# Gate and up products of a SwiGLU block by Strassen's algorithm, and the FFN walked group by group

## The chip, the core and the metric

The kernel runs on one core of a Trainium2 chip. TensorE (PE) multiplies, VectorE (DVE), ScalarE (ACT) and GpSimd (POOL) work elementwise, and transfers between HBM and the on-chip memory are issued by SyncE (SP). The metric is the device time of one execution in microseconds (us); the time of a kernel is the median of several runs.

## The reference, cut to what matters

One layer of a hybrid encoder: 2048 tokens, model width 1024, FFN width 2816 (22 blocks of 128). The first part (projections, two kinds of attention, a short convolution) is left alone by the change, but for the sizes of some buffers. The second part, on which the change works, is

```
x = x + y @ w_out[l]
x = x + swiglu(rmsnorm(x, ffn_norm_w[l]), w_gate[l], w_up[l], w_down[l])

def swiglu(x, w_gate, w_up, w_down):
    return (jax.nn.silu(x @ w_gate) * (x @ w_up)) @ w_down
```

## The kernel before

Tokens are handled in 4 groups of 512, in two halves of two groups. Every float32 product is made of three matmuls on split operands: high by high, high by low and low by high (`mm3`, L379 to L381). For the projections and for gate and up the parts are float16; for `w_down` they are float32r.

First comes a woven stage (`weave`, `fill`): projections, attention and the output projection of the first half are interleaved on TensorE by a clock of estimated costs. Then `ffn(0)` runs the FFN of the first half, `out_proj` the output projection of the second half with nothing beside it, and `ffn(1)` the FFN of the second half.

Within `ffn` the 22 FFN blocks f are taken two at a time. For each f and each of the half's two groups g, `hidden` (L379 to L381) makes gate and up: 8 slices of the width 1024, three matmuls each, with a 128x128 piece of the weight as the stationary operand and 512 tokens as the moving one, into a PSUM bank `acc`. ScalarE reads gate (`silu`, L1034), VectorE multiplies by up (`gated`, L1038), and the result is split into `gh` (ScalarE, L1041) and `gl` (VectorE, L1042). One pair later `down` (L1057 to L1059) multiplies these by `w_down`: six matmuls of 512 columns for each bank `sc`, of which there are three, and VectorE adds the bank to the residual `x1` (L1061). Weights of gate and up are scaled, cast and split once in `ffn(0)` (L249, L274 to L276) and stored as float16 in HBM (`wd`), from where `ffn(1)` fetches them (L236). `w_down` is loaded and split in each half (`load_down`, L310 to L314).

The order on TensorE is the order in which the program is written; in the FFN, and on the other engines everywhere, a scheduler sets it. All DMAs go through SP's one queue, in order.

Of the kernel before, what the change touches and what calls it, by code (L numbers as in the profile page):

```python
# [9 lines left out]
F32 = mybir.dt.float32  # L10
# [8 lines left out]
D = 1024  # L19
# [16 lines left out]
def f32(ap):  # L36
    return ap.bitcast(F32)
# [3 lines left out]
def trunk(ctx: ExitStack, tc: tile.TileContext, x, anw, w_in, qnw, knw, biasx, conv_w, onw, w_out,  # L41
# [17 lines left out]
    wp = ctx.enter_context(tc.tile_pool(name="wp", bufs=8))  # L59
    xp = ctx.enter_context(tc.tile_pool(name="xp", bufs=6))  # L60
# [109 lines left out]
    def block(key):  # L170
# [13 lines left out]
        if key[0] == "gu":  # L184
            return SH_T, False, "f", [cols(w, every, 128 * key[1], 128) for w in (w_gate_k, w_up_k)]
# [121 lines left out]
    def load_down(f, low):  # L307

        raw = wp.tile([128, D], F32, name="wr", tag="wr", bufs=4)
        nc.sync.dma_start(raw, w_down[f * 128:(f + 1) * 128, :])  # L310
        hi = wp.tile([128, D], F32R, name="wh", tag="w16")
        nc.scalar.copy(hi, raw)
        lo = wp.tile([128, D], F32R, name="wl", tag="w16")
        low.tensor_tensor(lo, raw, f32(hi), ALU.subtract)  # L314
        return hi, lo
# [5 lines left out]
    def to_T(xn, hh, hl, t):  # L321

        cs = slice(t * 128, (t + 1) * 128)
        for i in range(2):
            p, bk = sc1()
# [15 lines left out]
    def gain_row(key):  # L341

        w = {"a": anw, "o": onw, "f": fnw}[key]
        gt = xp.tile([128, D], F32, name="gain", tag="gain", bufs=1)
        nc.sync.dma_start(gt, bass.AP(tensor=w.tensor, offset=w.offset, ap=[[0, 128], [1, D]]))
        if key not in GS:
# [6 lines left out]
            nc.vector.tensor_scalar(t, t, -1.0, float(2 * 127 + 9), op0=ALU.mult, op1=ALU.add)  # L353
# [155 lines left out]
    def proj_N(H, groups, units, use, prep=None):  # L509

        for g in groups:
            hh, hl = H.get(g, (None, None))
            for t in range(0, 4, 2):
# [3 lines left out]
                o, bk = acc()  # L517
# [192 lines left out]
    def open_av():  # L710
        return bank("av", 1, 2 * HD)
# [146 lines left out]
    def out_proj(H, groups, W, prep, rows):  # L858

        for g in groups:  # L860
            for cb in range(4):
# [13 lines left out]
                if g == groups[-1] and cb in (1, 2) and len(groups) > 1:  # L875
                    yield from rows.ahead()

    def ffn_rows(H, groups):
        def fetch(g, b):
            xt = xp.tile([128, D], F32, name="xf", tag="xt")  # L880
            last_row[where(g)[0]] = nc.sync.dma_start(xt, x1d[g * 4 + b])
            return xt

        return Rows(H, groups, fetch, normed("f"))

    HF = [{}, {}]
    last_row = [None, None]
    frows = [ffn_rows(HF[i], groups) for i, groups in enumerate(HALVES)]


# [8 lines left out]

    def fill():  # L900
# [3 lines left out]
        rows = [x_rows(H[0], HALVES[0]), x_rows(H[1], HALVES[1]), y_rows(H[2], HALVES[0])]  # L904
        for half, groups in enumerate(HALVES):
# [19 lines left out]
        yield from out_proj(H[2], HALVES[0], W, rows[2], frows[0])  # L925
# [4 lines left out]
    FFN = [("gu", f) for f in range(NF)]  # L930
    stream = Weights(HALF * 2 + OUT * len(HALVES[0]) + FFN + OUT * len(HALVES[1]) + FFN)
    def hidden(u, h):

        (wh, wl), (hh, hl) = u, h
        o, bk = acc()
        bk.done = True
        yield from mm3(o, lambda k: wh[:, k, :], lambda k: wl[:, k, :], lambda k: hh[:, k, :],
                       lambda k: hl[:, k, :], KT)
        return o

# [77 lines left out]
    fp = ctx.enter_context(tc.tile_pool(name="fp", bufs=1))  # L1018

    def ffn(half, groups):  # L1020
        X1 = {}
        H = HF[half]

        def product(u, g):
            steps = hidden(u, H[g])
            while True:
                try:
                    next(steps)
                except StopIteration as e:
                    return e.value  # L1030

        def silu(f, o):
            sg = fp.tile([128, GRP], F32, name="sg", tag="sg", bufs=3)
            nc.scalar.activation(sg, o, AF.Silu, scale=descale(("gu", f), 0))  # L1034
            return sg

        def gated(f, sg, o):
            nc.vector.scalar_tensor_tensor(sg, o, descale(("gu", f), 1), sg, op0=ALU.mult, op1=ALU.mult)  # L1038
# [101 lines left out]
```

## Time and profile before

| | |
|---|---|
| median of 3 runs (lowest, highest) | 2697.33 us (2696.89, 2701.96) |
| the profiled execution | 2698.59 us, of which the trace's span is 2696.8 us |
[...]
| TensorE busy, share of the span | 94% |
| VectorE, ScalarE, GpSimd | 54%, 40%, 15% |

The span is the time from the first to the last instruction. A matmul's time in the trace covers its way through the pipeline and overlaps the next one's, so what a matmul costs in a stream is the distance between the starts of successive ones.

### The profile page before, as it was taken

The numbers are of one execution on the slowest core, as the hardware profiler recorded it, in microseconds if no ns is written. First come the engines' busy times: TensorE is split into PE (matmuls) and PEld (weight loads), VectorE is DVE, ScalarE is ACT, GpSimd is POOL, SyncE is SP. The second block draws the span as 40 slices with busy tenths as digits, with TensorE's granted clock in tenths as the row PEclk, the third lists the DMA queues.
The fourth block names the chain that finished last, engine by engine and source line by source line (L and its number), as shares of the span: only waits on it lengthen the run. The fifth ranks groups of instructions, "written<-read, shape, count | busy, mean of one in ns | idle before, by whom it ended". The sixth has DMA issues, their size and how long they took to land.

```text
span 2696.8 us, 41816 instructions
## 1 busy us (share of the span) xinstructions
PE 2526.3 (94%) x16258; PEld 1687.1 (63%) x16258; DVE 1458.7 (54%) x3343; ACT 1074.8 (40%) x1994; POOL 398.8 (15%) x469
## 2 busy tenths in 40 slices
PE   6998889998799888979999999999999999999999
PEld 4477766666686677745555555557865555555556
DVE  6478777689988977834444334334332333223233
ACT  5575756666456776752333333321121111111110
POOL 2234331102312122121111111110000000000000
PEclk9999999999999999989999999999999999999999
DMA  7443444533321356472222233222651111111101
GB/s 260 133 131 100 132 134 143 142 110 124 105 81 43 97 152 198 120 268 105 94 94 94 94 103 113 90 102 107 223 194 39 47 47 51 66 47 48 47 24 63
DMA packets 245350, 294.31 MB, mean 109 GB/s; under 512 B 77472, under 2 KB 194208, under 8 KB 245152
## 3 DMA queue, kind: packets, MB, share of 16 engines
q1 hardware_dynamic: 245152, 291.65, 33.5%
q8 instruction: 127, 2.08, 0.3%
q14 instruction: 71, 0.58, 0.1%
HBM read 199.30 MB, written 92.27 MB: 108 GB/s over the span
## 4 chain that ended last, share of the span: by engine, by line
PE 38%; DMA 4%; issue 4%; DVE 2%; POOL 1%; ACT 1%; SPq 1%; POOLq 0%; DVEq 0%; ACTq 0%
PE acc L381 7%; PE acc L380 7%; PE acc L379 7%; PE sc L1057 5%; PE sc L1058 5%; PE sc L1059 5%; DMA x1d<-xs 1%; POOL w L276 1%; DMA wr<-in_w_down 1%; DMA wr<-in_w_up 1%; DMA xf<-x1d 0%; PE sc L329 0%; DVE gl L1042 0%; DVE x L1061 0%; DVE wl L314 0%
## 5 line engine op out<-in xcount | busy, mean ns | idle before, releaser
L381 PE MATMUL acc<-hh,w 128*128 128x512 f16 x1728 | 656.3, 380 | 0.8 <-POOL w L276 0.8
L379 PE MATMUL acc<-hh,w 128*128 128x512 f16 x1728 | 656.5, 380 | 0.4 <-ACT hh L332 0.4
L380 PE MATMUL acc<-hl,w 128*128 128x512 f16 x1728 | 656.4, 380 | 0.1
L1038 DVE SCALAR_TENSOR_TENSOR sg<-acc,ds,sg 128x512 f32<-128x512 f32 x88 | 66.0, 750 | 622.9 <-PE acc L381 548.8
L379 PE MATMUL acc<-w,hh 128*128 128x256 f16 x1408 | 391.6, 278 | 5.8 <-ACT w L275 4.2
L380 PE MATMUL acc<-w,hh 128*128 128x256 f16 x1408 | 391.5, 278 | 1.8 <-POOL w L276 1.8
L381 PE MATMUL acc<-w,hl 128*128 128x256 f16 x1408 | 391.0, 278 | 1.5 <-DVE hl L333 0.8
L1061 DVE TENSOR_TENSOR x<-sc,x 128x512 f32<-128x512 f32 x352 | 241.2, 690 | 200.9 <-PE sc L1059 194.1
L381 PEld LDWEIGHTS <-w 128*128 128x128 f16 x1728 | 169.1, 98 | 206.4 <-issue 2.0
L379 PEld LDWEIGHTS <-w 128*128 128x128 f16 x1728 | 169.3, 98 | 184.9 <-issue 7.2
L380 PEld LDWEIGHTS <-w 128*128 128x128 f16 x1728 | 169.2, 98 | 180.3 <-issue 1.1
L1057 PE MATMUL sc<-wh,gh 128*128 128x512 f32 x704 | 278.7, 396 | 3.0 <-DVE x L1061 3.0
L1058 PE MATMUL sc<-wl,gh 128*128 128x512 f32 x704 | 274.4, 390 | 0.0
L1059 PE MATMUL sc<-wh,gl 128*128 128x512 f32 x704 | 274.3, 390 | 0.0
L276 POOL TENSOR_TENSOR w<-wr,w 128x1024 f16<-128x1024 f32 x76 | 163.4, 2164 | 550.6 <-ACT w L275 515.0
L669 DVE SCALAR_TENSOR_TENSOR wtl<-tp,wth 128x512 f16<-128x512 f32 (+3 forms) x384 | 198.4, 532 | 41.8 <-ACT wth L664 40.4
L733 DVE TENSOR_TENSOR_SCAN re<-re,zero 128x512 f32<-128x512 f32 (+3 forms) x160 | 192.6, 1203 | 39.7 <-ACT re L730 39.2
L664 ACT ACTIVATE wth<-tp 128x512 f16<-128x512 f32 (+3 forms) x384 | 173.6, 476 | 87.3 <-PE tp L660 86.0
L1041 ACT CAST gh<-sg 128x512 fp32r<-128x512 f32 x88 | 54.3, 617 | 385.3 <-DVE sg L1038 385.3
L274 ACT ACTIVATE wr<-wr,wsc 128x1024 f32<-128x1024 f32 x76 | 84.4, 1146 | 202.0 <-DVE wsc L263 201.8
L380 PEld LDWEIGHTS <-hh 128*128 128x128 f16 x1408 | 140.5, 100 | 31.7 <-issue 5.5
L679 PE MATMUL av<-v,wth 128*128 128x128 f16 x1104 | 144.0, 224 | 16.3 <-ACT yu L694 16.2
(168 smaller groups left out, 3724.3 us busy)
## 6 DMA issues: line engine op xcount, KB each, us to landing
w<-wd SPq DMA_DIRECT2D x92, 512.0 KB, 4.0
wd<-w SPq DMA_DIRECT2D x76, 512.0 KB, 2.9
wr<-in_w_down SPq DMA_DIRECT2D x44, 512.0 KB, 4.4
q<-qd SPq DMA_DIRECT2D x192, 64.0 KB, 2.3
wr<-in_w_gate SPq DMA_DIRECT2D x22, 512.0 KB, 4.5
wr<-in_w_up SPq DMA_DIRECT2D x22, 512.0 KB, 5.3
xt<-in_x SPq DMA_DIRECT2D x16, 512.0 KB, 5.2
wr<-in_w_in SPq DMA_DIRECT2D x16, 512.0 KB, 5.1
```

The source lines that it names most:

```text
L276: nc.gpsimd.tensor_tensor(w[:, 1, :], raw, w[:, 0, :], ALU.subtract)
L379: nc.tensor.matmul(o, sh(k), mh(k), start=(k == 0), stop=False)
L380: nc.tensor.matmul(o, sh(k), ml(k), start=False, stop=False)
L381: nc.tensor.matmul(o, sl(k), mh(k), start=False, stop=(k == n - 1))
L664: nc.scalar.activation(wh[:, b0 * 128:b1 * 128], tp[:, :(b1 - b0) * 128], AF.Copy, scale=WSC)
L669: nc.vector.scalar_tensor_tensor(wl[:, s], tp[:, :(b1 - b0) * 128], WSC, wh[:, s], op0=ALU.mult, op1=ALU.subtract)
L679: nc.tensor.matmul(av, wh[:, i * 128:(i + 1) * 128], vs[i], start=first and i == 0, stop=last and i == n - 1 > 0)
L733: nc.vector.tensor_tensor_scan(re, re, zero.to_broadcast([128, N]), 1.0 if b == T else e[:, 0:1], ALU.mult, ALU.add)
L1057: nc.tensor.matmul(o, gh[:, cs], wh[:, cc], start=st, stop=False)
L1058: nc.tensor.matmul(o, gh[:, cs], wl[:, cc], start=False, stop=False)
L1059: nc.tensor.matmul(o, gl[:, cs], wh[:, cc], start=False, stop=en)
L1061: nc.vector.tensor_tensor(x1, o, x1, ALU.add)
```

## The change

Strassen's algorithm (in Winograd's form, with 15 additions) multiplies 2x2 blocks with seven products of half size instead of eight. A unit is now one pair p of FFN blocks, one group g and one of gate and up (i = 0, 1). The blocks of the weight are two halves of the width 1024 by two FFN blocks; those of the activations are two halves of the width by two halves of the group's tokens. Each of the seven products is 4 slices by three matmuls of 128x128 by 256 columns (`product`).

- Sums of weight blocks are made in the first group (`unit_make`: two scalings, four sums on VectorE, seven casts on ScalarE, seven subtractions on GpSimd) into tiles `wa` (four operands, 1 MB) and `wb` (three), which are stored in HBM and fetched again for the other three groups (`unit_fetch`). The scale comes from `unit_norm` and from `unit_scale`, which has two tiny matmuls on TensorE.
- Sums of activation blocks are made once for each group (`operands`).
- The products are summed on VectorE when they leave PSUM (`a2` to `b2`): seven operations of 256 columns a unit, `s1` being copied by ScalarE.
- The FFN goes through the four groups one after the other, 11 pairs each; `w_down` is loaded and split in each. Output projection, normalisation and operands of the next group run a few steps at a time beside the products (`run_side`), in other PSUM banks: `av` (one) for the projection, `tp` (two) for transposes and for `down`.
- On-chip pools shrink (`wp` 8 to 4 buffers, `xp` 6 to 4); the FFN's order on TensorE is now the written one.

```diff
-    wp = ctx.enter_context(tc.tile_pool(name="wp", bufs=8))
-    xp = ctx.enter_context(tc.tile_pool(name="xp", bufs=6))
+    wp = ctx.enter_context(tc.tile_pool(name="wp", bufs=4))
+    xp = ctx.enter_context(tc.tile_pool(name="xp", bufs=4))
...
-                o, bk = acc()
+                o, bk = acc() if stream.paced else bank("av", 1)
...
+    def unit_tiles():
+        return (fp.tile([128, 4, 2, 512], F16, name="wa", tag="wa", bufs=2),
+                fp.tile([128, 3, 2, 512], F16, name="wb", tag="wb", bufs=2))
+
+    def unit_make(p, i):
...
+        for r in (r1, r2):
+            nc.scalar.activation(r, r, AF.Copy, scale=sc)
+        a11, a12, a21, a22 = r1[:, :512], r1[:, 512:], r2[:, :512], r2[:, 512:]
+
+        def parts(dst, f):
+            nc.scalar.copy(dst[:, 0, :], f)
+            nc.gpsimd.tensor_tensor(dst[:, 1, :], f, dst[:, 0, :], ALU.subtract)
...
+        parts(wa[:, 0], a11)
+        s1 = made(ALU.add, a21, a22)
+        s2 = made(ALU.subtract, s1, a11)
+        parts(wa[:, 1], s2)
+        parts(wb[:, 0], s1)
+        parts(wa[:, 3], a12)
+        parts(wa[:, 2], made(ALU.subtract, a11, a21))
+        parts(wb[:, 1], a22)
+        parts(wb[:, 2], made(ALU.subtract, a12, s2))
...
+    def product(o, A, B):
+        for k in range(4):
+            ks = slice(k * 128, (k + 1) * 128)
+            ah, al = A[:, 0, ks], A[:, 1, ks]
+            bh, bl = B[:, 0, k, :], B[:, 1, k, :]
+            nc.tensor.matmul(o, ah, bh, start=k == 0, stop=False)
+            nc.tensor.matmul(o, ah, bl, start=False, stop=False)
+            nc.tensor.matmul(o, al, bh, start=False, stop=k == 3)
...
+        def a2(self):
+            o = self.mul(1, sc1)
+            self.u2 = q("u2", 1)
+            nc.vector.tensor_tensor(self.u2, o, self.s1, ALU.add)
...
+        def a5(self):
+            o = self.mul(2, sc1)
+            self.c_of(o, self.u3, 1, 1)
+            nc.vector.tensor_tensor(self.u2, o, self.u2, ALU.add)
...
+        for n, u in enumerate(units):
+            g, p, i = u
+            new = n < n1 - 2
+            if new and units[n + 2] not in norms:
+                norms[n + 2] = unit_norm(*units[n + 2][1:])
+            if g not in BS:
+                run_all(sides[units[n - 1][0]])
+            U = Unit(g, p, i, made.pop(u))
+            U.a1()
+            if last is not None:
+                last.b1()
+                last.b2()
+            U.a2()
+            per = 3 if n >= n1 else 2
+            run_side(g, per)
+            U.a3()
+            run_side(g, per)
+            U.a4()
+            if new:
+                unit_scale(*units[n + 2][1:], norms.pop(n + 2))
+            if n + 2 < len(units):
+                nu = units[n + 2]
+                made[nu] = unit_make(*nu[1:]) if new else unit_fetch(*nu[1:])
+            prev = (g, p - 1) if p else (order[order.index(g) - 1], NP - 1)
+            if prev in G:
+                down(*prev, (0, 1) if i == 0 else (2, 3))
+            if i == 1:
...
+                DW[g, p] = [load_down(f) for f in (2 * p, 2 * p + 1)]
+            if n + 4 < n1:
+                unit_load(*units[n + 4][1:])
+            U.a5()
+            run_side(g, per)
+            last = U
```

On VectorE, before, late in the second half: `wl` is the low part of a `w_down` block, `sg` the gated product, `gl` its low part, `x1` the residual.

```order
L1061 TENSOR_TENSOR x1_24122<-sc_27500,x1_24122 128x512
L314 TENSOR_TENSOR wl_27744<-wr_27740,wh_27742 128x1024
L314 TENSOR_TENSOR wl_27750<-wr_27746,wh_27748 128x1024
L1038 SCALAR_TENSOR_TENSOR sg_27537<-acc_27539,ds37_21801,sg_27537 128x512
L1042 TENSOR_TENSOR gl_27566<-sg_27537,gh_27565 128x512
L1038 SCALAR_TENSOR_TENSOR sg_27594<-acc_27596,ds37_21801,sg_27594 128x512
```

The same engine in the changed kernel, in the last group, at the end of a unit with i = 1; `c`, `u2` and `u3` are sums of products.

```order
L1271 TENSOR_TENSOR x1_30907<-tp_32785,x1_30907 128x512
L312 TENSOR_TENSOR wl_32797<-wr_32793,wh_32795 128x1024
L312 TENSOR_TENSOR wl_32803<-wr_32799,wh_32801 128x1024
L1231 TENSOR_TENSOR c_32818<-sc_32805,u3_32739 128x256
L1227 TENSOR_TENSOR u2_32724<-sc_32805,u2_32724 128x256
L1198 SCALAR_TENSOR_TENSOR sg_32609<-sg_32609,ud6_1_20309,c_32818 128x256
L1231 TENSOR_TENSOR c_32850<-sc_32837,u3_32739 128x256
```

Both parts of `wl` still stand ahead of the reads of the next product's bank; that bank is now half as wide in columns, and there are seven of them a unit.

On SP, before, in the second half, for one pair: four fetches of 512 KB of prepared gate and up weights (`w`), and the two raw `w_down` blocks (`wr`).

```order
L236 DMA w_26380<-wd_0_20772 128x2048
L236 DMA w_26382<-wd_1_20773 128x2048
L236 DMA w_26498<-wd_0_20917 128x2048
L236 DMA w_26500<-wd_1_20918 128x2048
L310 DMA wr<-in_w_down 128x1024 x2
```

In the changed kernel, in the last group, for one pair: the operand tiles of gate (`u_0`) and of up (`u_1`), and `wr` as before.

```order
L1017 DMA wa<-u_04_18816 128x4096
L1017 DMA wb<-u_03_18817 128x3072
L1017 DMA wa<-u_14_19080 128x4096
L308 DMA wr<-in_w_down 128x1024 x2
L1017 DMA wb<-u_13_19081 128x3072
```

The fetches are larger (1.05 MB and 0.79 MB), and `wr` now stands directly behind a `wa` and ahead of a `wb`. A pair here serves one group, before it served two.

## Rows read from the trace of the kernel before

**Rows 1.** The page's first part: busy time, share of the span, instructions.

```profile
span 2696.8 us, 41816 instructions
PE 2526.3 (94%) x16258; PEld 1687.1 (63%) x16258; DVE 1458.7 (54%) x3343; ACT 1074.8 (40%) x1994; POOL 398.8 (15%) x469
```

**Rows 2.** Stretches: length, busy time by engine, granted clock, DMA share, GB/s.

```profile
1170.00:1200.00 30.00, 13.33 (x59) 8.68 (x58) 17.91 (x50) 21.10 (x31) 7.44 (x4) 0.72 0.84 302
1200.00:1885.00 685.00, 681.98 (x3109) 396.00 (x3107) 263.89 (x502) 195.78 (x267) 96.73 (x45) 1.00 0.30 103
1885.00:2002.00 117.00, 111.94 (x940) 92.25 (x939) 42.86 (x91) 23.23 (x42) 0.00 (x0) 1.00 0.66 219
2002.00:2012.00 10.00, 5.61 (x32) 4.73 (x31) 8.83 (x20) 4.90 (x10) 0.00 (x0) 0.83 0.70 284
2012.00:2697.00 685.00, 679.91 (x3095) 396.75 (x3093) 208.10 (x286) 77.30 (x108) 0.00 (x0) 1.00 0.14 48
```

**Rows 3.** The page's costliest groups: busy time, mean ns, idle before, releaser.

```profile
L1038 DVE SCALAR_TENSOR_TENSOR sg<-acc,ds,sg 128x512 f32<-128x512 f32 x88 | 66.0, 750 | 622.9 <-PE acc L381 548.8
L1061 DVE TENSOR_TENSOR x<-sc,x 128x512 f32<-128x512 f32 x352 | 241.2, 690 | 200.9 <-PE sc L1059 194.1
```

**Rows 4.** Timeline, TensorE: first and last of 45 matmuls, then of 68.

```profile
2044.84 0.38 PE L379 MATMUL acc<-hh,w 128*128 128x512 f16 x1
...
2054.34 0.38 PE L381 MATMUL acc<-hh,w 128*128 128x512 f16 x1
2084.64 0.39 PE L1057 MATMUL sc<-wh,gh 128*128 128x512 f32 x1
...
2099.83 0.39 PE L1058 MATMUL sc<-wl,gh 128*128 128x512 f32 x1
```

**Rows 5.** Timeline, TensorE and its weight loads: first and last of 46 matmuls.

```profile
1904.98 0.27 PE L379 MATMUL acc<-w,hh 128*128 128x256 f16 x1
1904.98 0.10 PEld L380 LDWEIGHTS <-hh 128*128 128x128 f16 x1
...
1909.89 0.27 PE L379 MATMUL acc<-w,hh 128*128 128x256 f16 x1
```

**Rows 6.** Groups by form, VectorE, 1220 to 1800 us.

```profile
L1042 DVE TENSOR_TENSOR gl<-sg,gh 128x512 fp32r<-128x512 f32 x38 | 31.4, 825 | 17.4 <-ACT gh L1041 17.3
L314 DVE TENSOR_TENSOR wl<-wr,wh 128x1024 fp32r<-128x1024 f32 x18 | 22.0, 1225 | 23.8 <-ACT wh L312 23.3
L842 DVE TENSOR_TENSOR yt<-yt,yry 128x1024 f32<-128x1024 f32 x8 | 9.8, 1224 | 0.2
L263 DVE TENSOR_SCALAR wsc<-wsc 128x2 int32<-128x2 int32 x17 | 2.9, 169 | 0.6
```

**Rows 7.** Groups by form, VectorE, 1050 to 1150 us: 256 columns from PSUM.

```profile
L669 DVE SCALAR_TENSOR_TENSOR wtl<-tp,wth 128x256 f16<-128x256 f32 x32 | 13.3, 414 | 0.0
```

**Rows 8.** Groups by form, ScalarE (1220 to 1800 us), then GpSimd (whole span).

```profile
L274 ACT ACTIVATE wr<-wr,wsc 128x1024 f32<-128x1024 f32 x34 | 37.2, 1140 | 161.0 <-DVE wsc L263 160.8 <-DVE ds L266 0.2
L249 ACT ACTIVATE junk<-wr 128x1024 bf16<-128x1024 f32 x32 | 33.8, 1057 | 48.6 <-DMA wr<-in_w_gate 34.8 <-DMA wr<-in_w_up 13.8
L275 ACT CAST w<-wr 128x1024 f16<-128x1024 f32 x34 | 33.6, 1034 | 0.0
L579 POOL TENSOR_TENSOR qs<-qk 128x512 f32<-128x512 f32 x32 | 36.4, 1138 | 41.0 <-ACT qk L577 40.8
```

**Rows 9.** DMA: `w_down` loads to landing; a burst of loads; the page's sixth part.

```profile
DMA to landing us min/median/max: 3.1/3.3/3.5
1996.00:2008.00 12.00, 7.61 (x43) 4.20 (x41) 10.10 (x27) 4.96 (x9) 0.00 (x0) 1.00 1.02 408
wr<-in_w_gate SPq DMA_DIRECT2D x22, 512.0 KB, 4.5
```

**Rows 10.** Stretches with VectorE near full in attention; a stretch with TensorE empty.

```profile
1080.00:1100.00 20.00, 19.34 (x205) 16.24 (x205) 19.18 (x81) 17.65 (x43) 3.08 (x7) 1.00 0.60 169
1050.00:1100.00 50.00, 46.51 (x483) 39.85 (x480) 44.33 (x180) 39.28 (x97) 10.54 (x22) 0.97 0.66 198
1180.00:1185.00 5.00, 0.00 (x0) 0.00 (x0) 3.88 (x14) 4.87 (x9) 2.35 (x2) 0.50 0.63 233
```

More of the change, by code (lines that the diff above doesn't have):

```diff
@@ new lines, in trunk, with unit_load, unit_norm @@
+    UD = {}
+    UW = {}
+    UR = {}
+    srcs_u = (w_gate_k, w_up_k)
+    def unit_load(p, i):
+        UR[p, i] = raws = []
+        for f in (2 * p, 2 * p + 1):
+            raw = wp.tile([128, D], F32, name="wr", tag="wr", bufs=4)
+            nc.sync.dma_start(raw.rearrange("p (k c) -> p k c", k=KT), srcs_u[i][:, :, 128 * f:128 * f + 128])
+            raws.append(raw)
+    def unit_norm(p, i):
+        ss = small(2, "ws", BF16)
+        for j, raw in enumerate(UR[p, i]):
+            with nc.allow_low_precision(reason="a bound, to a factor of two"):
+                nc.scalar.activation(junk(), raw, AF.Square, accum_out=ss[:, j:j + 1])
+        return ss
@@ new lines, in unit_scale @@
+    def unit_scale(p, i, ss):
+        o, bk = bank("av", 1) if not stream.paced else tpb()
+        bk.done = True
+        for j in range(2):
+            nc.tensor.matmul(o[:, 0:1], ones, ss[:, j:j + 1], start=j == 0, stop=j == 1)
+        t = small(1, "wt")
+        sc = consts.tile([128, 1], F32, name=f"us{p}_{i}")
+        ds = consts.tile([128, 1], F32, name=f"ud{p}_{i}")
+        nc.vector.tensor_scalar(t.bitcast(I32), o[:, 0:1].bitcast(I32), 24, None, op0=ALU.logical_shift_right)
+        nc.vector.tensor_scalar(t.bitcast(I32), t.bitcast(I32), -1.0, 203.0, op0=ALU.mult, op1=ALU.add)
+        nc.vector.tensor_scalar(sc.bitcast(I32), t.bitcast(I32), 23, None, op0=ALU.logical_shift_left)
+        nc.vector.reciprocal(ds, sc)
+        nc.vector.tensor_scalar(ds, ds, INV["f"], None, op0=ALU.mult)
+        UD[p, i] = sc, ds
@@ L898, in later, with beside_of, unit_first @@
         waiting.sort(key=lambda w: w[0])
+    def beside_of(steps, more, every=8):
+        for n, c in enumerate(steps):
+            yield c
+            if n % every == every - 1:
+                yield from islice(more, 1)
+        yield from more
+    def unit_first():
+        for u in ((0, 0), (0, 1)):
+            unit_load(*u)
+        yield 0.0
+        yield 0.0
+        ss = [unit_norm(*u) for u in ((0, 0), (0, 1))]
+        yield 0.0
+        yield 0.0
+        for u, v in zip(((0, 0), (0, 1)), ss):
+            unit_scale(*u, v)
     def fill():
@@ L929, in trunk @@
     OUT = [("o", cb) for cb in range(4)]
[L930 to L939, printed above, removed]
+    stream = Weights(HALF * 2 + OUT * NG)
     def weave():
@@ new lines, in trunk @@
+    NP = NF // 2
+    order = [g for groups in HALVES for g in groups]
+    units = [(g, p, i) for g in order for p in range(NP) for i in range(2)]
+    def product(o, A, B):
+        for k in range(4):
+            ks = slice(k * 128, (k + 1) * 128)
[4 more added lines that the diff above has]
+            nc.tensor.matmul(o, al, bh, start=False, stop=k == 3)
@@ new lines, in proj_side, with operands_side @@
+    def proj_side(g):
+        H = {}
+        yield from out_proj(H, [g], stream, y_rows(H, [g]))
+    def operands_side(g):
+        yield from operands(g, s_tile, tpb)
+    second = HALVES[1]
+    sides = {}
+    for n, g in enumerate(order):
+        steps = []
+        if n == 0:
+            steps.append(y_side())
+        if n + 1 < len(order):
+            nxt = order[n + 1]
+            if nxt in second:
+                steps.append(proj_side(nxt))
+            steps.append(operands_side(nxt))
+        sides[g] = chain.from_iterable(steps)
@@ L1110 @@
+    with tc.manual_schedule(engines={mybir.EngineType.PE}):
+        ffn()
 def kernel(**inputs):
```

296 lines of the change are left out of this document (196 added, 100 removed).

## The prediction, made before the changed kernel ran

> **What bounds the kernel now.** The first part of the page gives TensorE 94% of the span and VectorE 54% [rows 1]. An average says little where stages differ, so I read the FFN in stretches. From 1200 to 1885 us and from 2012 to 2697 us TensorE is busy 682 and 680 of 685 us at full granted clock, VectorE 264 and 208 [rows 2]: these stretches are TensorE's, and every matmul fewer shortens them. Between and ahead of them lie three weaker places: 1170 to 1200 us, where TensorE is busy 13.3 of 30 us at a clock of 0.72; 2002 to 2012 us, 5.6 of 10; and the bare output projection from 1885 us, busy 112 of 117 [rows 2]. The groups by line confirm who waits: VectorE sat idle 549 us for gate and up products before its L1038, and 194 us for `down` banks before L1061 [rows 3].
>
> **What a matmul costs** is the distance of starts. For float16 with 512 columns it is (2054.34 - 2044.84)/44 = 0.2159 us, for float32r with 512 columns (2099.83 - 2084.64)/67 = 0.2267 us [rows 4]. For 256 columns, each with a weight load of its own, it is (1909.89 - 1904.98)/45 = 0.1091 us [rows 5]. So half the columns cost half the time, though a load of 0.10 us stands beside each.
>
> **The change, step by step.**
>
> *Products.* 88 results of gate, and as many of up (L1038 ran 88 times [rows 3]), took 8 x 3 matmuls each: 176 x 24 = 4224, times 0.2159 = 912 us. Now 4 groups x 11 pairs x 2 units x 7 products x 12 = 7392 matmuls, times 0.1091 = 806.5 us. That is 105.5 us less. `down` keeps 352 x 6 = 2112 matmuls [rows 3]; the projections and transposes keep their number. Upper bound of the new price: the saving is gone at 912/7392 = 0.123 us a matmul; nothing in rows 5 hints at it.
>
> [...]
>
> *Start of the FFN: -7 us.* Before, 1170 to 1200 us lost 16.7 us idle and some 4 us to the low clock [rows 2], 20 in all. Now the first product waits, after the last projection, for five small VectorE operations (0.17 each [rows 6], 0.9), two scalings of 1.14, half a cast of 1.03 and a GpSimd subtraction of 1.14 [rows 8]: 4.9 us. Then `unit_scale` for unit 2 stands in TensorE's order after a4 of unit 0. Its raw weights can only be loaded when unit 0's sixth subtraction has freed a buffer (4.9 + 5 x 1.14 = 10.6 us), land 4.5 us later [rows 9] and need two squares of 1.06 [rows 8]: about 18 us, where TensorE gets there at 12. Together some 13 us lost. Bounds: 5 (buffers free in time) to 25.
>
> *First group: +35 us.* TensorE has 22 x 84 x 0.1091 + 10 x 48 x 0.2267 = 310 us. VectorE has, for 22 units: 154 reads of 256 columns at 0.42 (a read of that width took 0.414 [rows 7]), 65; 88 weight sums of 512 columns at 0.69 [rows 3] to 0.83 (GpSimd running beside it [rows 6]), 61 to 73; 44 multiplications at 0.45, an estimate from rows 3 and 7, 20; 22 `gl`, 15 to 18; 80 residual sums at 0.69, 55; 22 `wl` at 1.22 [rows 6], 27; 22 scale chains of 0.9, 20; eight normalised blocks of `y` at 4.5, an estimate (1.22 for the product [rows 6], two reductions at 0.69, eleven small ones at 0.17), 36; the next group's operands 15. Sum 314 to 329 us: as much as TensorE. VectorE had 39% in this part of the FFN [rows 2]; now its order and TensorE's hold each other. Attention is the nearest place where both are nearly full: VectorE was busy 44.3 of 50 us and, at best, 19.2 of 20 [rows 10]. At those shares 329 us of work takes 371 or 343 us, so 33 to 61 us more than TensorE's 310. Where the casts run late the chain for `wl` is also behind. With sums at the lower price it would be 314/0.96 = 327, +17. I take 35; bounds 0 to 61. The first units are worst, since `y_side` falls on them alone.
>
> *Later groups: +10 us.* TensorE needs 168 x 0.1091 + 48 x 0.2267 = 29.2 us a pair, VectorE some 17 (14 reads of 0.42, four multiplications, two `gl`, eight sums of 0.69, two `wl`). The risk is order. `wl` stands on VectorE ahead of the read of a5's bank, and SP sends `wr` only behind a `wa` that waits until a4 has freed its buffer. From a4's end: 1.05 MB of `wa` and two `wr` of 0.52 MB at 0.41 MB/us [rows 9] take 5.1 us, plus 2.0 us of latency (3.3 us for one load [rows 9], less 1.3 of transfer), 7.1; cast 1.04, `wl` 1.22: 9.4; two reads of a5's bank, 10.2. TensorE wants that bank back, for a2 of the next unit, after four `down` banks of 1.36 and four products of 1.31: 10.7 us. So it just fits, 0.5 us to spare; each us of lateness beyond that costs one a pair, 33 pairs. I take 0.3 a pair; bounds 0 and 3 (loads landing at 4.5 instead of 3.3 us, for both).
>
> *Beside the products: +16 us.* The projection has one bank now. Of its 16 blocks of 48 matmuls in the two sides most are followed directly by the next, which waits for a VectorE read of 0.75 [rows 3] and its way there. I take 0.6 each, 10 us, bounds 0 to 19; transposes, which share two banks with `down`, 6 more. In exchange the bare projection and 2002 to 2012 us lose their gaps, 5 + 4.4 idle and some 1.5 of low clock [rows 2]: -11.
>
> *Group ends and tail: +11 us.* Three times residual tiles must be stored before the next are loaded, and `wr` stands behind them on SP: two more landings of 3.3, of which I count 2.7 us as seen, 8; at the very end `gl` of the last pair has no product to hide it, 3.
>
> *At nothing:* the 66 refetched units (1.84 MB each) and the doubled `w_down`, since 4.7 MB in 29.2 us is 0.16 MB/us of the 0.41 that a burst reached [rows 9]; the casts of ScalarE, about 280 us of the first group's 310; and the smaller `wp` and `xp`, which the attention stage covers by loading one block ahead, up to 10 us if that cover is gone.
>
> Sum: -105.5 - 7 + 35 + 10 + 16 - 11 + 11 = -52 us on a span of 2697 [rows 1], 2645. The profiled execution is 1.8 us over its span and 1.3 over the median of the runs, so against the median the prediction is about 2645 us. A measurement of this kernel can tell about 0.2%, 5 us, from no change.
>
> **The rivals.**
>
> *The saving arrives almost whole (0.22).* VectorE slips under the products (first group +5), the sides cost 8 and the ends 7: -105.5 - 18 + 20, 2593 us, with 2580 to 2612 as its own range. For it: rows 4 and 5 leave no doubt on the products, and the bare projection's gaps are certain. Against it: VectorE's sum of the first group.
>
> *The second `w_down` half comes late everywhere (0.16).* If raw weights land 2.5 us later than worked out above (as when two other transfers share the queue, or the order of `wa` and `wr` on SP holds them), VectorE stands at `wl` while a5's bank is full, TensorE stops before a2, and every one of 43 pairs pays 2.0 us: 2645 - 10 + 86 = 2721 us, slower. It decides from 52 + 10 = 62 us over 43 pairs, 1.4 us a pair. For it: only 0.5 us is spare, and wherever TensorE stopped for 5 us its clock fell to 0.50 [rows 10], which adds to the price. Against it: single loads of `w_down` never took over 3.5 us in the second half [rows 9].
>
> *The weight load is not hidden at 256 columns (0.02).* If it were added, a matmul would cost 0.10 + 0.109 us [rows 5], and the products 7392 x 0.209 = 1545 us, 633 more than before: about 3280 us. Rows 5 are a stream of just that form and show 0.109.
>
> **How the numbers follow.** My forecast (2612 to 2690) has 0.52, the two ends 0.22 and 0.16, the load 0.02; 0.06 lies within 5 us of the old time, and 0.02 below 2580. Faster: 0.22 + 0.52 + 0.02 = 0.76; same 0.06; slower 0.18. The range for 8 in 10 runs from the fast rival's lower edge, 2580, to just over the old time, 2703, since the slower rival starts there. Forecast and fast rival are both faster; alone they would give 2580 to 2690.
>
> **What would show it.** Products: about 7392 matmuls of 128x256 with starts 0.109 us apart, and 29 to 30 us a pair in the last group. First group: VectorE busy over 85% there, TensorE waiting for it. Later groups: waits of matmuls for `u2` or `c` reads under 1 us a pair; if they are 2 us, with VectorE idle before `wl` for ScalarE or DMA, the second rival is right. Start: a gap of about 5 us before the first product, another at the scale matmul of unit 2. Wrong altogether: 256-column starts further apart than 0.115 us in the FFN, or attention ending over 10 us later than it did.

## The result, and the profile after

The changed kernel takes 2828.9 us (median of four runs, 2823.2 to 2834.7), the kernel before on the same chip 2697.1 us: a ratio of 1.0485 (95% interval 1.046 to 1.051). It is slower by 132 us; the forecast was 2645 us, 184 less than measured.

First the page's first part, the answer to [rows 1]:

```profile
span 2827.6 us, 50313 instructions
PE 2491.9 (88%) x19448; PEld 2017.8 (71%) x19448; DVE 1886.5 (67%) x4181; ACT 1249.7 (44%) x2380; POOL 591.3 (21%) x635
```

TensorE is busy 34 us less than before, not 105 us as its products alone would have it. Part went back in a lower granted clock, 0.951 of full speed in the mean where the kernel before had 0.982: at 0.50, from 1172.93 to 1175.07 us, the starts of 11 matmuls of 256 columns stood 0.21 us apart, against 0.109 at 1.00. The stretches show where (columns as in [rows 2]; the clock is a mean over the stretch; the first stretch is the first group, from the copy of `s1` in unit 0 to that in unit 22, then groups two, three and four):

```profile
1186.50:1671.30 484.80, 355.95 (x2342) 287.30 (x2342) 342.72 (x661) 249.65 (x414) 233.77 (x166) 0.85 0.55 181
...
1671.00:2080.00 409.00, 380.32 (x2830) 324.33 (x2829) 213.60 (x386) 86.41 (x149) 19.70 (x14) 0.97 0.51 170
2080.00:2484.00 404.00, 378.86 (x2829) 324.04 (x2827) 212.48 (x386) 86.74 (x149) 18.81 (x14) 0.98 0.47 159
2484.00:2828.00 344.00, 337.13 (x2434) 287.25 (x2431) 189.32 (x348) 65.91 (x112) 0.00 (x0) 1.00 0.47 159
```

The fourth group has nothing beside it, and there the plan works: 22 units of 14.69 us, at a granted clock of 1.00. Its products stand as far apart as [rows 5] said. TensorE's timeline, first and last of 25 matmuls, 24 distances: (2703.95 - 2701.33)/24 = 0.109 us.

```profile
2701.33 0.27 PE L1171 MATMUL sc<-hl,wb 128*128 128x256 f16 x1
...
2703.95 0.27 PE L1171 MATMUL sc<-bx,wb 128*128 128x256 f16 x1
```

The first group is the trouble. In 485 us TensorE is busy 356 and VectorE 343: neither is near full, as VectorE was to be. TensorE's longest waits there (for what, released by which engine and line; us in all, times, longest):

```profile
PE tp L1267 <- ACT wh L310: 24.2, 8, 5.8
PE tp L908 <- DVE xf L372: 22.4, 1, 22.4
PE tp L1267 <- ACT gh L1245: 20.1, 7, 9.1
PE sc L1170 <- DVE u L1227: 17.8, 8, 3.3
PE av L967 <- ACT junk L959: 17.1, 2, 12.7
PE tp L1268 <- DVE wl L312: 13.5, 9, 5.0
```

There is no one wait to remove: `wh` and `wl` (the split of `w_down`), operands of the next group (`xf`), the gated product (`gh`), reads of banks (`u`), the scale matmul (`junk`). The third place to look is how long the operations take, against [rows 3, 6 to 8]. VectorE by form, 1412 to 1640 us, then GpSimd:

```profile
L1271 DVE TENSOR_TENSOR x<-tp,x 128x512 f32<-128x512 f32 x43 | 29.2, 686 | 14.2 <-PE tp L1269 14.2
L997 DVE TENSOR_TENSOR S<-wr 128x512 f32<-128x512 f32 x22 | 23.7, 1079 | 15.5 <-ACT wr L988 15.4
L1198 DVE SCALAR_TENSOR_TENSOR sg<-sg,ud,c 128x256 f32<-128x256 f32 x21 | 14.6, 693 | 0.2
L1231 DVE TENSOR_TENSOR c<-sc,u 128x256 f32<-128x256 f32 x32 | 13.4, 419 | 19.3 <-PE sc L1172 18.4 <-ACT sg L1196 0.9
L997 DVE TENSOR_TENSOR S<-wr,S 128x512 f32<-128x512 f32 x11 | 13.3, 1205 | 0.0
L312 DVE TENSOR_TENSOR wl<-wr,wh 128x1024 fp32r<-128x1024 f32 x10 | 12.2, 1225 | 14.7 <-ACT wh L310 14.7
L1246 DVE TENSOR_TENSOR gl<-sg,gh 128x512 fp32r<-128x512 f32 x10 | 12.2, 1261 | 1.7 <-ACT gh L1245 1.7
L997 DVE TENSOR_TENSOR S<-S,wr 128x512 f32<-128x512 f32 x11 | 9.7, 882 | 0.0
```

```profile
L993 POOL TENSOR_TENSOR wa<-S,wa 128x512 f16<-128x512 f32 x22 | 32.3, 1476 | 8.4 <-ACT wa L992 8.1
L993 POOL TENSOR_TENSOR wb<-S,wb 128x512 f16<-128x512 f32 x22 | 30.3, 1376 | 50.0 <-ACT wb L992 50.0
```

Operations that read a PSUM bank cost what was predicted (`x` 0.686, `c` 0.419 us). Most of those that read two tiles of the on-chip memory do not: the sums `S` and `gl` took 0.88 to 1.26 us where I had 0.69 to 0.83, the multiplication `sg` 0.69 where I had 0.45, and GpSimd's subtractions 1.24 to 1.48 (in four groups, of which two are shown) where I had 1.14. Only `wl` kept its 1.22. Taken one by one from the timelines of the first group, 25 of its 100 `S` and `gl` met no GpSimd operation, and each took 0.68 or 0.69 us; the other 75 overlapped one and took 0.68 to 1.65, 1.14 in the mean.

Stage by stage, against the prediction's own terms:

| stage | predicted | measured | difference |
|---|---|---|---|
| last `av` matmuls of attention (before 1151.21) | 1151.2 | 1161.8 | +10.6 |
| from there to the first product | 10 (5 of projection, 4.9) | 9.6 | 0 |
| first product to that of the second group | 345 and 8 of the second gap | 498.4 | +145 |
| groups two and three | 2 x 395 | 812 | +22 |
| group four and the end | 345 | 344 | -1 |

For the second to fourth row the first product was read at 1171.46 us and that of unit 22 at 1669.82. The 395 are 321 for products and `down` (11 x 29.2), 59 for half of the bare projection without its gaps [rows 2] and half of the 31 that I had added for banks, order and ends. These stage figures were set apart after the result and sum to 2649, 4 us above the forecast; the differences sum to 177 of the 183 us that separate forecast and span. Nearly all of it is the first group.

### The profile page after: what moved, and what is told of

It is laid out like the page before. It is cut to its first block, busy times and chain, and to the rows that moved or that the text cites. A ratio compares the mean times of both kernels' runs of the same rounds, so it can differ in the third digit from the quotient of the medians.

```text
span 2827.6 us, 50313 instructions
## 1 busy us (share of the span) xinstructions
PE 2491.9 (88%) x19448; PEld 2017.8 (71%) x19448; DVE 1886.5 (67%) x4181; ACT 1249.7 (44%) x2380; POOL 591.3 (21%) x635
## 5 line engine op out<-in xcount | busy, mean ns | idle before, releaser
L1271 DVE TENSOR_TENSOR x<-tp,x 128x512 f32<-128x512 f32 x352 | 242.5, 690 | 212.7 <-PE tp L1269 212.5
L1267 PE MATMUL tp<-wh,gh 128*128 128x512 f32 x704 | 296.4, 421 | 61.7 <-ACT wh L310 24.2
L378 PE MATMUL acc<-w,hh 128*128 128x256 f16 x1152 | 325.1, 282 | 3.8 <-ACT w L273 3.8
L379 PE MATMUL acc<-w,hh 128*128 128x256 f16 x1152 | 324.7, 282 | 1.8 <-POOL w L274 1.8
L1268 PE MATMUL tp<-wl,gh 128*128 128x512 f32 x704 | 286.8, 407 | 13.6 <-DVE wl L312 13.5
L1269 PE MATMUL tp<-wh,gl 128*128 128x512 f32 x704 | 285.0, 405 | 1.1 <-DVE gl L1246 1.1
L733 DVE TENSOR_TENSOR_SCAN re<-re,zero 128x512 f32<-128x512 f32 (+3 forms) x160 | 191.4, 1196 | 39.8 <-ACT re L730 39.4
L1267 PEld LDWEIGHTS tp<-wh,gh 128*128 128x128 f32 x704 | 138.4, 197 | 97.9 <-ACT wh L310 27.1
L1171 PE MATMUL sc<-bx,wb 128*128 128x256 f16 x704 | 192.3, 273 | 0.0
L1170 PE MATMUL sc<-bx,wb 128*128 128x256 f16 x704 | 192.3, 273 | 0.0
L1172 PE MATMUL sc<-bx,wb 128*128 128x256 f16 x704 | 192.3, 273 | 0.0
L1171 PEld LDWEIGHTS <-wa 128*128 128x128 f16 x1408 | 140.0, 99 | 44.1 <-issue 26.0
L1268 PEld LDWEIGHTS tp<-wl,gh 128*128 128x128 f32 x704 | 138.6, 197 | 44.2 <-DVE wl L312 18.1
L1269 PEld LDWEIGHTS tp<-wh,gl 128*128 128x128 f32 x704 | 138.5, 197 | 35.9 <-DVE gl L1246 5.0
```

The lines of the kernel that those rows point to most:

```text
L378: nc.tensor.matmul(o, sh(k), mh(k), start=(k == 0), stop=False)
L379: nc.tensor.matmul(o, sh(k), ml(k), start=False, stop=False)
L733: nc.vector.tensor_tensor_scan(re, re, zero.to_broadcast([128, N]), 1.0 if b == T else e[:, 0:1], ALU.mult, ALU.add)
L1170: nc.tensor.matmul(o, ah, bh, start=k == 0, stop=False)
L1171: nc.tensor.matmul(o, ah, bl, start=False, stop=False)
L1172: nc.tensor.matmul(o, al, bh, start=False, stop=k == 3)
```

## The experiments

Three theories of the first group stood against each other, with one on attention beside them. R: raw `w_down` blocks share a ring of four buffers with the raw units, arrive late and stop TensorE at `wh`, `wl`. B: side work comes in bunches, ahead of what TensorE waits for. C: VectorE and GpSimd slow each other. In each run the length of the first group is that from the copy of `s1` in unit 0 to that in unit 22 (after: 484.8 us), and a pair is the mean over units 10 to 20 (after: 42.0 us, against 29.4 in the last group). Each experiment is one execution, but for e11 (four) and e12 (six). The four executions of the changed kernel lay 12 us apart, so a few us between two kernels settle nothing by themselves.

**e1: other buffers for raw `w_down` blocks.**

```diff
-                DW[g, p] = [load_down(f) for f in (2 * p, 2 * p + 1)]
+                DW[g, p] = [load_down(f, "w16" if n < n1 - 2 else "wr") for f in (2 * p, 2 * p + 1)]
```

> The changed kernel, but in the first group the raw w_down blocks use buffers of their own (the idle ones of the projection weights) instead of sharing four with the raw gate and up weights. Theory R (raw buffers: the second raw w_down block cannot be loaded until a unit's weights are made, so its parts come late and VectorE and TensorE stop behind them): the later pairs of the first group (41.9 us each in the changed kernel, 29.4 in the last group) fall to about 33, some 60 us less in all, about 2770. Theory C (VectorE and GpSimd slow each other): pairs stay over 39 us, at most 15 us less. Theory B (the work beside the first ten units is bunched and its latency is not hidden): the first ten units stay at 259 us.

Measured: 2822.1 us; first group 478.8 us, a pair 40.5. The waits for `wh` and `gh` are gone, and another has taken their place. TensorE's longest wait in e1:

```profile
PE sc L1170 <- DVE u L1227: 75.7, 11, 14.9
```

R alone falls: what was waited for there was late anyway for VectorE.

**e2: side work spread.** Four yields ahead of and five behind each `y_norm`, six steps of pause behind each fetch and normalisation of operands.

```diff
+        yield from pause(6)
...
+            yield from pause(6)
```

> The changed kernel, with pauses between the steps of the work beside the products: nine more steps for each normalised block of y, six more between load and norm and between norm and transposes of the operands (no instruction more or less). Theory B (bunching, unhidden latency): the first ten units fall from 259 to about 200 us, the two later group changes lose some 20 us less each: about 2730. Theories R and C: the work only moves to later units, the first group as a whole (485 us to unit 22) stays within 15 us, the later group changes may gain.

Measured: 2784.4 us. First group 468.7 us, groups two and three 392.4 and 390.6 (408.6 and 403.8 in the changed kernel), which are the 395 that I had predicted. So B explains the 22 us of the later groups, and 16 of the first.

**e3: no low parts.** GpSimd's subtraction becomes a memset; the low parts of the weight operands are left out as zero.

```diff
-            nc.gpsimd.tensor_tensor(dst[:, 1, :], f, dst[:, 0, :], ALU.subtract)
+            nc.gpsimd.memset(dst[:, 1, :], 0.0)
```

> The changed kernel, with the low parts of the weight operands not computed: GpSimd fills them with zero instead of subtracting, so 154 subtractions of 1.2 to 1.5 us become short fills that read nothing. Theory C (GpSimd and VectorE slow each other): VectorE's 512-column sums return from 1.05 to 0.69 us, its gl from 1.26 to 0.69, and the first group gets 50 us or more shorter. Theories R and B: VectorE gets faster, but the first group gains under 20 us.

Measured: 2776.6 us; first group 432.1 us, a pair 37.2. The sums are back at the price of [rows 6]'s undisturbed operations (VectorE by form, 1390 to 1590 us, then GpSimd):

```profile
L997 DVE TENSOR_TENSOR S<-wr 128x512 f32<-128x512 f32 x22 | 15.1, 686 | 7.5 <-ACT wr L988 7.5
...
L1198 DVE SCALAR_TENSOR_TENSOR sg<-sg,ud,c 128x256 f32<-128x256 f32 x21 | 10.1, 482 | 0.4
...
L1246 DVE TENSOR_TENSOR gl<-sg,gh 128x512 fp32r<-128x512 f32 x10 | 6.5, 688 | 1.8 <-ACT gh L1245 1.8
```

```profile
L993 POOL MEMSET wa<- 128x512 f16 x44 | 21.2, 526 | 27.2 <-PE av L967 22.2 <-ACT wb L992 4.9
```

GpSimd still writes the same tiles. Seven of the ten `gl` overlap a memset and take 0.68 or 0.69 us; the sums of this stretch meet no GpSimd operation at all. The edit also takes work from GpSimd, which is busy 107 us in the group instead of 234, so the 53 us are the turns and that work together.

**e4: e1 and e2 together.**

> The edits of the first two together. If R and B are both right the gains add: first ten units near 190 us, later pairs near 33, group changes 20 us shorter each, about 2670. If C is what holds the first group, it stays over 440 us and the time over 2760.

Measured: 2748.1 us; first group 435.8 us, a pair 39.8. Both together take 49 us from the first group, where singly they took 6 and 16: each had uncovered the other's wait. The group and the time lie between the two forecasts. With less in the way, the turns of the two engines are seen plainly. VectorE at the start of the first group, then GpSimd:

```profile
1169.12 0.69 DVE L1004 TENSOR_TENSOR S<-wr 128x512 f32<-128x512 f32 x1 [1.74 <-ACT wr L995]
1169.85 1.53 DVE L1004 TENSOR_TENSOR S<-S,wr 128x512 f32<-128x512 f32 x1
1171.30 1.64 DVE L1004 TENSOR_TENSOR S<-wr 128x512 f32<-128x512 f32 x1
1172.86 1.64 DVE L1004 TENSOR_TENSOR S<-wr,S 128x512 f32<-128x512 f32 x1
```

```profile
1169.62 2.77 POOL L1000 TENSOR_TENSOR wa<-wr,wa 128x512 f16<-128x512 f32 x2 [8.43 <-ACT wa L999]
1172.35 1.60 POOL L1000 TENSOR_TENSOR wb<-S,wb 128x512 f16<-128x512 f32 x1
1173.91 1.60 POOL L1000 TENSOR_TENSOR wa<-S,wa 128x512 f16<-128x512 f32 x1
```

The first sum takes 0.69 us, most of it before GpSimd starts. Soon both engines start something every 1.56 us (1171.30 and 1172.86; 1172.35 and 1173.91), and each record is longer than the work alone. Undisturbed, such operations start 0.61 us apart on VectorE (e6, below) and 1.12 us apart on GpSimd (this run, at 1175.47 and 1176.59), so a turn of both is a little shorter than the two one after the other, 1.73.

**e5: e4 and e3 together** (low parts left out as zero).

> e4 with the GpSimd subtraction replaced by a memset, so the low parts of the weight operands are left out as zero. R and B are removed by e4's edits, C by the memset. If the three together are the whole loss of the first group, its pairs come near TensorE's own time: 30 to 32 us a pair in units 10 to 20 (e4: 39.8), units 0 to 10 under 180 us (e4: 204), the span about 2746 - 85 = 2660 us. If something else holds the first group (the scale of the next unit in TensorE's order, ScalarE's casts), pairs stay at 36 or above and the span at 2700 or above.

Measured: 2672.5 us, 18.7 less than a run of the kernel before on the same chip (2691.2). The first group:

```profile
1181.10:1541.30 360.20, 326.92 (x2342) 272.14 (x2342) 284.45 (x661) 245.36 (x415) 105.14 (x162) 0.96 0.71 245
```

R, B and C together are worth 125 us of the group, while singly they gave 6, 16 and 53, sum 75. A pair is 33.9 us, more than the 30 to 32 expected: at least 2 us a pair are none of the three. The same 2342 matmuls are busy 327 us here and 356 in the changed kernel, at a mean granted clock of 0.96 against 0.85: up to 29 of the 125 us are matmuls that ran longer at the lower clock.

**e6: the subtractions on VectorE**, from e4.

```diff
-            nc.gpsimd.tensor_tensor(dst[:, 1, :], f, dst[:, 0, :], ALU.subtract)
+            nc.vector.tensor_tensor(dst[:, 1, :], f, dst[:, 0, :], ALU.subtract)
```

> e4 with the seven subtractions of a unit moved from GpSimd to VectorE; nothing is left out. C (the two engines take turns where both read the on-chip memory): sums go back to about 0.68 us, VectorE has 11.1 + 11.4 + 14 x 0.68 = 32 us of work a pair and nothing beside it, so pairs fall from 39.8 to 33 or 34 us though VectorE does more; span about 2746 - 65 = 2680 us. Rival (VectorE is just overloaded, and the long durations are waits for operands that the trace counts in): 9.5 us more work a pair, so 45 to 49 us a pair, span 2800 or above.

Measured: 2753.0 us; first group 446.8 us, a pair 41.3. Neither came: the sums did go back to about 0.69 us, and the pairs did not fall. TensorE's timeline and VectorE's, the end of one pair, show what stopped it:

```profile
1424.78 0.27 PE L1179 MATMUL sc<-bx,wb 128*128 128x256 f16 x1
1432.10 0.37 PE L1177 MATMUL sc<-hh,wa 128*128 128x256 f16 x1 [7.05 <-DVE u L1234]
```

```profile
1426.63 0.68 DVE L1278 TENSOR_TENSOR x<-tp,x 128x512 f32<-128x512 f32 x1
1427.23 2.35 DVE L312 TENSOR_TENSOR wl<-wr,wh 128x1024 fp32r<-128x1024 f32 x2
1429.49 0.68 DVE L1000 TENSOR_TENSOR wb<-S,wb 128x512 f16<-128x512 f32 x1
1430.10 0.68 DVE L1000 TENSOR_TENSOR wb<-wr,wb 128x512 f16<-128x512 f32 x1
1430.70 0.68 DVE L1000 TENSOR_TENSOR wb<-S,wb 128x512 f16<-128x512 f32 x1
1431.30 0.41 DVE L1238 TENSOR_TENSOR c<-sc,u 128x256 f32<-128x256 f32 x1
1431.63 0.41 DVE L1234 TENSOR_TENSOR u<-sc,u 128x256 f32<-128x256 f32 x1
```

The two reads that free a5's bank stand behind both `wl` and three low parts; TensorE waits 7.05 us for the second. This is the place that my second rival named, the read of a5's bank behind `wl`, but not its cause: VectorE does not stand there for late weights, it has no idle time in these rows. Its own block of work is ahead of the reads.

**e8: e6, with the making of a unit in three pieces** between the next unit's products.

```diff
+            step(m)
             U.a2()
+            step(m)
...
+            run_all(m)
             U.a4()
```

> e6 with the sums and subtractions of a unit written in three pieces between the next unit's products (after b2, a2 and a3) in place of one block after a4, and the raw weights loaded one unit later. If in e6 the block of 11 VectorE operations still stands ahead of reads of products, pairs fall by 1 to 3 us against e6, to 31 to 32 us, span about 2660 us. If VectorE's sum of 32 us a pair binds, it stays within 0.7 us a pair of e6.

Measured: 2723.0 us; first group 413.7 us, a pair 39.2. The edit, which also loads the raw weights one unit later, was worth 33 us of the group, though only 2.1 a pair in units 10 to 20. There VectorE is now busy 178 of 196 us, 91%, within the 89 to 96% that the prediction took from attention.

**e9 and e10: e8 with all seven subtractions of a unit on GpSimd, then with four there and three on VectorE.** In e10 (e9 has GpSimd in every call):

```diff
+        def parts(dst, f, low=nc.gpsimd):
...
+        parts(wb[:, 0], s1, nc.vector)
+        parts(wb[:, 2], made(ALU.subtract, a12, s2), nc.vector)
...
+        parts(wb[:, 1], a22, nc.vector)
```

> e8 with the seven subtractions of a unit back on GpSimd. VectorE's sum of units 0 to 20 was 350 us in e8; without the 280 subtractions of 0.68 it would be 160 us less, were it not for the turns. If taking turns costs as much as doing the work oneself (C), pairs of units 10 to 20 stay within 2 us of e8's 39.2, sums take over 1.1 us again, and the span lies between 2705 and 2740 us. If the order of the pieces was the whole trouble in e4, pairs fall to 33 or 34 us and the span to about 2670 us.

> e8 with four of the seven subtractions of a unit (those of wa) on GpSimd and three (wb) on VectorE. VectorE's own work is 22.5 + 6 x 0.68 = 26.6 us a pair and GpSimd's 8 x 1.15 = 9.2 us. If both have room then, pairs fall from 39.2 to 34 to 36 us and the span to 2670 to 2700 us. If every us that GpSimd works is taken from VectorE, the two sum to 36 us and pairs stay at 38 to 40 us, the span at 2710 to 2730 us.

Measured: e9 2756.6 us, first group 438.9, a pair 41.1; e10 2729.6 us, 416.5, 39.3. Windows of the first group in e8, e9 and e10:

```profile
1178.70:1592.40 413.70, 345.28 (x2363) 283.74 (x2361) 370.89 (x812) 250.87 (x420) 42.30 (x22) 0.93 0.64 217
```

```profile
1187.30:1626.20 438.90, 352.42 (x2343) 286.68 (x2343) 357.79 (x661) 247.37 (x416) 233.03 (x166) 0.90 0.61 200
```

```profile
1182.80:1599.30 416.50, 344.42 (x2342) 281.78 (x2342) 361.65 (x723) 248.56 (x415) 154.38 (x103) 0.92 0.63 209
```

GpSimd is busy 191 us more in e9 than in e8 and VectorE only 13 us less. With the work in pieces, GpSimd's help made the group 25 us longer. The pairs of both came out as the theory of turns had them, e9's time 17 us above its range.

**e11 to e13: is it VectorE's sum?** In the written program, e11 is e10 with the four blocks of `y` for the last group moved to the second; e12 moves the other four as well (each four one group later) and loads the raw weights of units 2 and 3 into idle buffers; e13 moves all eight out of the first group in the changed kernel as it was. The last lines are e12's alone.

```diff
-        if n == 0:
-            steps.append(y_side())
+        if n in (1, 2):
+            steps.append(y_side(second[n - 1]))
...
-                unit_load(*units[n][1:])
+                unit_load(*units[n][1:], "w16")
```

> e10 with the normalisation of y for the last group moved from the first group into the second. It takes four blocks of 4.5 us, 18 us, from VectorE where it is fullest. If VectorE's sum sets the first group's length, the group is 12 to 18 us shorter than in e10, and the second group at most 4 us longer: the span falls by 10 to 16 us. If the order of single waits sets it, the gain is under 5 us. Against before (2692 to 2697 us) it comes out between 2660 and 2700 us.

> e11 with the other four blocks of y moved as well (to the second group; those of the last group to the third), and the raw weights of units 2 and 3 loaded into idle buffers of their own, so that the second gap at the start (12.6 us) closes. If VectorE's sum sets the first group's length, it falls from 406 to about 406 - 18 - 10 = 378 us, the span to 2690 us, level with before. If single waits set it, only the 10 us of the start come, span about 2707 us.

> The changed kernel with y moved out of the first group as in e12, nothing else. If VectorE's sum sets the length, the group falls by about 36 us from 485 to 450. If y's bunched block stops TensorE in units 2 to 9 beyond its own work, units 0 to 10 fall by over 40 us (243.6 to under 204) and pairs of units 10 to 20 stay at 41 to 43 us. The second group gets 12 more steps of side work; its length may change by up to 10 us either way.

Measured: e11 2719.6 us (ratio to before 1.0114, 1.0091 to 1.0138), first group 406.1; e12 2708.7 us (1.0067, 1.005 to 1.0084), 401.7; e13 2816.7 us, 482.1. The window of the first group and TensorE's longest waits there, in e13:

```profile
1185.90:1668.00 482.10, 358.86 (x2354) 289.87 (x2355) 320.09 (x596) 246.11 (x408) 226.04 (x163) 0.86 0.52 173
```

```profile
PE tp L1267 <- ACT wh L310: 34.3, 9, 8.4
PE tp L908 <- DVE xf L372: 25.2, 1, 25.2
PE sc L1170 <- DVE u L1227: 20.8, 9, 3.5
```

The edits did not do all that they were to do. On VectorE the order is the scheduler's, and it drew blocks of `y` forward from the second group into unit 21, the last of the first group: three in e11 and in e12, four in e13. VectorE's `y` there in e13:

```profile
L842 DVE TENSOR_TENSOR yt<-yt,yry x4: 1215/1218/1224, 1645.3 to 1661.4; 128x1024 f32<-128x1024 f32 x4
```

Unit 21 took 23.0 us in e13 and 14.7 in the changed kernel. So e13 moves half of `y`, and gathers the other half: VectorE is relieved of 22.6 us in the group, units 0 to 10 are 10.9 us shorter, the last two units 6.8 longer, the waits for `wh` grew from 24 to 34 us, and the group is 2.7 shorter. In e11 VectorE has only 7.9 us less and the group is 10.4 shorter, between the two forecasts (12 to 18, under 5). e12 has 24.5 us less on VectorE than e11 and gains 4; its first unit fell from 17.5 to 6.5 us, but unit 2 grew from 19.6 to 32.7.

What answers the question for the changed kernel is a stretch without `y`, of which it does all eight blocks by unit 4. This is its window of units 10 to 20:

```profile
1430.00:1640.00 210.00, 167.94 (x1086) 135.38 (x1085) 136.05 (x241) 109.47 (x179) 96.79 (x72) 0.89 0.50 163
```

VectorE is busy 65% of it, and a pair still takes 42.0 us. So VectorE's sum does not set the length there. With the work in pieces it may: units 10 to 20 took 196.8, 178.8 and 171.8 us in e10, e11 and e12, with VectorE busy 171.6, 151.2 and 141.8. But transposes of the next group's operands moved to earlier units as well, so that is not shown.

**e7, e7b, e7c: attention.** The kernel before with the smaller rings of the changed one.

```diff
-    xp = ctx.enter_context(tc.tile_pool(name="xp", bufs=6))
+    xp = ctx.enter_context(tc.tile_pool(name="xp", bufs=4))
...
-                w = wp.tile([128, 2, D], F16, name="w16", tag="w16")
+                w = wp.tile([128, 2, D], F16, name="w16", tag=ring(key), bufs=size(key))
```

> The kernel before, with xp of 4 buffers in place of 6 and wp of 8 as it was. If the smaller xp makes attention end 10.6 us late, the last av matmul stands at 1160 to 1163 us (before 1151.4) and the span grows by about 10 us or more. If wp does it, the last av stays at 1151 to 1153 us.

> The kernel before, with 4 buffers in place of 8 for the scaled weights of projections and output projection; the FFN's weights have a ring of 5 of their own. If the smaller wp makes attention end late, the last av matmul stands at 1158 to 1163 us (before 1151.4). If not, it stays at 1151 to 1154 us, and the lateness comes from the operands and scales that the changed kernel weaves into that stage. The FFN of this kernel may be slower for its smaller ring; only the stage up to 1170 us is read.

> The kernel before with both rings of the attention stage as in the changed kernel: xp of 4 buffers and 4 buffers of scaled weights (the FFN has its own ring of 5). If the two smaller rings together make attention late, its last av matmul stands at 1159 to 1163 us (before 1151.4). If they only add, 2.2 + 1.8, it stands at 1155 us, and the rest of the 10.6 us comes from what the changed kernel weaves into that stage besides.

Measured: the last `av` matmuls stand 2.2, 1.9 and 1.4 us later than before (e7 2697.8 us, e7b 2704.4, e7c 2703.5 in all). The rows of the changed kernel and of e7c, which answer to 1151.21 before:

```profile
1161.82 0.39 PE L678 MATMUL av<-v,wth 128*128 128x128 f16 x4
```

```profile
1152.61 0.39 PE L685 MATMUL av<-v,wth 128*128 128x128 f16 x4
```

The rings explain 1.4 of 10.6 us. In the twelve kernels made from the changed one that end stood between 1159.2 and 1167.4 us. At nine tenths of these matmuls the changed kernel was 8 us late already, and the rest came while operands and scales of the first group are woven in. Which edit makes it is open.

## Why the prediction was wrong, point by point

*What held.* The price of a product (0.109 us) and the weight load (0.10 us) hidden beside it; the pairs of the last group (29.4 us for 29.2 and 0.3); the end; the gap before the first product (4.2 us for 4.9). The gap at the scale of unit 2 was there too, but its two matmuls waited 4.4 and 12.7 us where I had 8 in all. The turns of the subtractions that free the raw buffers are the smaller part of that, since e3, without these subtractions, still waited 13.8: the second raw block stands on SP's queue behind the stores of unit 1's operands (1189.22 and 1190.33 us, the block at 1190.70). For the later groups e2 shows the price right once their side work is spread; in the written order it comes in bunches, 22 us more, which "Beside the products: +16" did not hold.

*What failed: "First group: +35 us".* It is the step that makes the answer wrong: the group took 498 us where TensorE's own 310, this term and the second gap gave 353. The loss of 180 us beside the gap lies outside the term's own bounds of 0 to 61. Three of its assumptions fell.

First, the prices. I took weight sums at "0.69 to 0.83 (GpSimd running beside it)", from the mean of [rows 6]. That mean hid two kinds: of 38 `gl` 31 took 0.68 or 0.69 us and seven 1.22 to 1.65, and each of the seven stood beside one GpSimd operation, as here (VectorE, then GpSimd, in the kernel before):

```profile
1270.33 1.22 DVE L1042 TENSOR_TENSOR gl<-sg,gh 128x512 fp32r<-128x512 f32 x1 [0.61 <-ACT gh L1041]
```

```profile
1268.60 2.41 POOL L843 TENSOR_TENSOR yt<-yt,gain 128x1024 f32<-128x1024 f32 x1 [14.79 <-PE sc L1059]
```

So the price of a collision was to be read before the change, and 154 new GpSimd operations were to be charged to VectorE. By itself this is the small part: VectorE was busy 343 us in the group where the sum had 314 to 329. How far it goes the runs show: turns of 1.56 us in e4, nearly the 1.73 of two whole operations; `gl` of 0.69 us beside memsets in e3; and in the changed kernel's first group 51 `x`, which read a PSUM bank, at 0.68 or 0.69 us beside GpSimd operations. What makes the two engines take turns, no run shows.

Second, the place of the work. Without the low parts the first group is 53 us shorter (e3), or 76 once R and B are gone (e4 to e5). Moving them to VectorE brings the sums back to about 0.69 us and gains nothing (e6), since it then has them itself. Beyond the start of the FFN the prediction charged these subtractions to no engine; there was no cover for them.

Third, the form of the estimate. I divided VectorE's sum by its share in attention, 89 to 96%. In the first group it is busy 71%, not the 85% that was to show, and TensorE 73%; in units 10 to 20 VectorE has 65%. Only with the making on VectorE in pieces (e8) does it come to 91% there. Two engines that each go in order, with ScalarE, GpSimd and one DMA queue between them, wait for each other by turns: remove one wait and the next in line stands there (e1), and the gains of several edits are more than the sum of their single ones (75 against 125 us). TensorE's matmuls themselves were up to 29 of the 125 us longer, at the lower mean clock (0.85 against 0.96). What the group still takes beyond TensorE's time when the three are gone (a pair 33.9 us in e5 against 29.4) has no cause shown.

*"At nothing".* Attention ended 10.6 us later; I had named up to 10 us for the smaller rings, but they explain 1.4 of them (e7c), and the rest is open.

*The rivals.* The saving almost whole had VectorE slip under the products; it does so in no run that makes the low parts. The late second half of `w_down` was right in kind, wrong in place: 14.69 us a unit in the last group, where it was to cost as in every pair; in the first, where I had not priced it by itself, TensorE stood 24 us for `wh`, at `down`. The load's rival was summed wrongly: its 633 us count from the products before, so against the forecast they are 739, and the time about 3384 us, not 3280. Nothing rests on it.

No complete version beat the kernel before. The best, e12, is 0.5 to 0.8% slower; its first group still takes 402 us, and the least that any run reached is e5's 360, with a part of the computation left out. Sharing one unit's operands between two groups, which would halve the making per unit of TensorE time, was not tried.

## What to carry to other kernels

Price a stage by its own engines' orders, not by their sums: where two engines at 70% wait for each other, look for the operations that stand ahead of what the other waits for. Before moving elementwise work to GpSimd, look in the trace for the longest, not the mean, of VectorE's operations beside a GpSimd one (`gl` before: 1.65 us, where the mean is 0.83), and charge that work to both. A saving on the full engine is worth only as much as the stage that must prepare it can deliver; here 105 us of products were saved over four groups, and one group that makes the operands lost more than that.

## What the runs showed of the hardware

Unexpected was the size of the turns: a float32 operation of 512 columns on two on-chip tiles goes from 0.69 to as much as 1.64 us on VectorE, and GpSimd's from 1.14 [rows 8] to 1.60 (e4), while in the changed kernel's first group reads of PSUM beside the same GpSimd work keep their 0.42 (`c`) and 0.69 us (`x`). Where VectorE's operation began first, it kept its time there: 18 sums `S` that began ahead of the GpSimd operation that overlapped them took 0.68 or 0.69 us, and ten such `wl` 1.21 to 1.23, the GpSimd operations beside these `wl` 1.62 to 2.12. The one `wl` that began behind took 1.58, and 57 `S` and `gl` that did took 0.68 to 1.65, 1.29 in the mean. Beside a GpSimd memset of 0.53 us `gl` kept 0.69 (e3).

The granted clock was lower where TensorE stood more: a mean of 0.80 over 1186 to 1430 us, where it stood 85 of 243 us, and 1.00 in the last group, where it stood 7 of 344. The prediction's fall to 0.50 was read in one stop [rows 10]; in the changed kernel a stop of 22.4 us from 1286.8 us had 0.50, and one of 13.5 us from 1952.6 us 0.69 in the mean.
